# A scatter-add of expert results, with and without a bound on its row numbers

## The chip, the cores and the metric

The kernel runs on one core of a Trainium2 chip. The metric is the device time of one execution in microseconds (us), taken as the median of several runs. TensorE is called PE in the profile, VectorE DVE, ScalarE ACT, GpSimd POOL and SyncE SP; the core's transfers run on 16 DMA engines.

## The reference

One layer of a decoder is computed for 512 prompt tokens and 32 sample tokens, 544 tokens in all. The part that matters here is its end, a mixture of experts: every token goes to two of 32 experts, and the two results, times their gates, are added to the residual stream.

```python
    expert_ids = g_idx * EXPERTS_PER_GROUP + e_idx
    gates = jnp.einsum('nk,nke->ne', w, jax.nn.one_hot(expert_ids, N_EXPERTS, dtype=jnp.float32)).astype(h.dtype)
    y = jnp.zeros_like(h)
    for e in range(N_EXPERTS):
        hid = jax.nn.silu(h @ lw['w_expert_gate'][e]) * (h @ lw['w_expert_up'][e])
        y = y + gates[:, e:e + 1] * (hid @ lw['w_expert_down'][e])
    return y

def channel_mixer(x, lw):
    ...
    return x + hier_moe(h, lw).reshape(B, S, D)
```

So there are 1088 pairs of token and expert. With the inputs that the reference draws (seed 0) the 32 experts get between 20 and 53 of them each.

## The kernel before

The first 700 us compute the mixer (projections, attention, convolution, memory, output projection) and write the residual stream to `out_y_all` in HBM. Its last columns of work give the router's scores, from which the kernel builds tables: for every expert 64 slots (`CAP`), filled from slot 0 on with the tokens that chose it.

Then the experts run in a loop, `for e in range(NE)`. For each one SP loads its weights as six transfers of 1 MiB (`expert_w`: two for the gate matrix, two for up, two for down), into a ring of 23 buffers. `wload` lets at most four of them be in flight: each load waits for the one issued four before it (`DEPTH`), and also until its buffer is free. PE multiplies the 64 gathered token rows by the gate and up matrices (L1516), gathers the next expert's rows in between (L1330), transposes the hidden activations (L1530) and multiplies by the down matrix (L1536). The 1024 output columns are worked on as two halves, the first in partitions 0 to 63 and the second in partitions 64 to 127, so partition 64 f + s holds half f of slot s.

DVE multiplies the result by the gates into `o`, which is `work[:, :512]` (L1539). There is one such tile for all experts. GpSimd then issues one indirect DMA (L1540), which adds the 128 rows of `o`, 2 KB each, to rows of `y2`, the view of `out_y_all` in half rows. The row numbers stand in one column of the table `ids2`, built by `rows_of` (L1401 to L1406): a slot with token t gets rows 2 t and 2 t + 1, and an empty slot gets rows from 1088 on, which no output is made of (`YROWS = NT + CAP`, and the host takes the first `NT` rows only):

```python
    f["dummy"] = (NT + 1 + p % CAP).astype(np.float32)[:, None]
...
        V.tensor_scalar(idz, idf, 0.5, cfs("dummy"), op0=ALU.is_lt, op1=ALU.mult)
        V.tensor_tensor(idf, idf, idz, op=ALU.add)
        return V.tensor_scalar(ids2[:, at:at + n], idf, 2.0, cfs("half"), op0=ALU.mult, op1=ALU.add)
```

Each scatter waits for the one before it to land, since both add to the same tensor. After the loop a second one treats experts with more than 64 tokens; its number of turns is read from a table (L1618), and with these inputs it is zero.

Of the kernel before, what the change touches and what calls it, by code (L numbers as in the profile page):

```python
# [17 lines left out]
ALU = mybir.AluOpType  # L18
# [7 lines left out]
NT = NP + NS  # L26
# [126 lines left out]
def build(tc, I, O, cols):  # L153
# [44 lines left out]
    def nm(s):  # L198
        cnt[0] += 1
        return f"{s}_{cnt[0]}"  # L200
# [1298 lines left out]
    def expert(xT, w, gc, idc2, after=None, mid=None, early=None):  # L1499
        with tc.issue_after(after.ins) if after is not None else nullcontext():  # L1500
            return expert_mm(xT, w, gc, idc2, mid, early)
# [8 lines left out]
    def expert_mm(xT, w, gc, idc2, mid, early):  # L1510
        pgt = pm.tile([P, 256], F32, name=nm("pg"), tag="pg")
        pup = pm.tile([P, 256], F32, name=nm("pu"), tag="pu")
        for ps, ws in ((pgt, w[0:2]), (pup, w[2:4])):
            for k in range(8):
                for f in range(2):
                    last = nc.tensor.matmul(ps[CAP * f:CAP * f + CAP], xT[:, k, :], ws[k // 4][:, k % 4, 256 * f:256 * f + 256],  # L1516
                                     start=(k == 0), stop=(k == 7))
            if early is not None and ps is pgt:
                early(last)
        if mid is not None:  # L1520
            with tc.issue_after(last.ins):
                mid()
        hs = work[:, 512:768]
        nc.scalar.activation(hs, pgt, AF.Silu)
        hp_ = work[:, 768:1024].rearrange("p (k q) -> p k q", k=2)
        nc.vector.tensor_tensor(hp_.rearrange("p k q -> p q k"), hs.rearrange("p (q k) -> p q k", k=2),  # L1526
                                pup.rearrange("p (q k) -> p q k", k=2), op=ALU.mult)
        ph = pm.tile([P, 2, P], F32, name=nm("ph"), tag="ph", bufs=1)
        for k in range(2):
            nc.tensor.transpose(ph[:, k, :], hp_[:, k], ident)  # L1530
        hT = hs.rearrange("p (f s) -> p f s", f=2)
        nc.vector.tensor_copy(hT, ph)  # L1532
        pd = pm.tile([P, 512], F32, name=nm("pd"), tag="pd")
        for kk in range(4):
            for f in range(2):
                last = nc.tensor.matmul(pd[CAP * f:CAP * f + CAP], hT[:, kk % 2, CAP * (kk // 2):CAP * (kk // 2) + CAP],  # L1536
                                 w[4 + kk // 2][:, kk % 2, 512 * f:512 * f + 512], start=(kk == 0), stop=(kk == 3))
        o = work[:, :512]
        nc.vector.tensor_scalar(o, pd, gc, None, op0=ALU.mult)  # L1539
        nc.gpsimd.indirect_dma_start(out=y2, out_offset=bass.IndirectOffsetOnAxis(ap=idc2, axis=0), in_=o,  # L1540
                                     in_offset=None, compute_op=ALU.add)
        return last

    def overflow_tables():
# [141 lines left out]
```

## Time and profile before

| | us |
|---|---|
| median of three runs | 1209.25 (1209.0 to 1210.12) |
| the profiled execution | 1208.48 |
| span of its trace, first to last instruction | 1206.7 |
| experts' stage, first scatter to last | 739.18 to 1199.04 |
| span: busy PE | 1117.8 (93%) |
| span: busy POOL | 289.7 (24%) |

The profile counts 327.77 MB moved, 310.10 MB of them by the queue of SP and 14.62 MB by the queue of GpSimd, which the scatters use. An instruction that issues a DMA shows on its engine only while the engine deals with the issue; the transfer itself shows in the DMA share and in the time to landing. The chain of waits on the page ends at the conditional loop behind the experts and so names only the last scatter. The stage has to be read from stretches, from SP's issues and from the waits in them.

### The profile page before, as it was taken

What the parts mean: (1) busy time and instruction counts of PE and PEld (TensorE: products, weight loads), DVE (VectorE), ACT (ScalarE), POOL (GpSimd) and SP (SyncE); (2) the same over time, 40 slices, a digit from 0 to 9 for tenths busy, and PEclk for the clock granted to TensorE, in tenths of its full rate; (3) what the DMA queues carried; (4) which work ended last, traced back from release to release, by engine and by line L of the source; (5) the groups of instructions that cost most, each with busy time, mean ns of one, the idle gap of its engine ahead of it and who ended that gap; (6) DMA issues with size and microseconds to landing.
All of it is one profiled execution on the core that took longest, in us unless ns stands there. A gap on an engine that the chain in (4) does not pass through costs nothing. (4 is left out here: it accounts for less than half of the span.)

```text
span 1206.7 us, 21730 instructions
## 1 busy us (share of the span) xinstructions
PE 1117.8 (93%) x8965; PEld 827.2 (69%) x8965; DVE 526.2 (44%) x974; ACT 295.2 (24%) x723; POOL 289.7 (24%) x465
## 2 busy tenths in 40 slices
PE   6999999988389999999999998999999999888885
PEld 6998888987375899999998853555555555444442
DVE  6634444695475799856432264211225121111111
ACT  7434444422032432244332232000000000000000
POOL 4352434650068320222222000111111111001111
PEclk9999999999589999999999998999999999999999
DMA  9953100596967997212319179999999999999996
GB/s 322 230 149 90 48 34 27 215 367 179 271 238 256 397 358 248 86 61 80 140 68 378 71 279 395 403 404 401 398 402 404 404 404 404 403 402 404 402 404 238
DMA packets 116036, 327.77 MB, mean 272 GB/s; under 512 B 13353, under 2 KB 70257, under 8 KB 88032
## 3 DMA queue, kind: packets, MB, share of 16 engines
q1 hardware_dynamic: 105520, 310.10, 68.1%
q0 software_dynamic: 7664, 14.62, 5.4%
q10 hardware_dynamic: 2752, 1.65, 0.5%
q8 instruction: 71, 1.16, 0.4%
q14 instruction: 29, 0.24, 0.1%
HBM read 310.18 MB, written 31.49 MB: 283 GB/s over the span
## 5 line engine op out<-in xcount | busy, mean ns | idle before, releaser
L1540 POOL DMA_INDIRECT out_y_all<-work,ids x32 | 49.9, 1559 | 452.5 <-DVE work L1539 413.4
L694 PE MATMUL mm<-hTh,hi 128*128 128x272 f32 x512 | 150.2, 294 | 7.1 <-DVE u L745 6.0
L696 PE MATMUL mm<-hTh,lo 128*128 128x272 f32 x512 | 149.1, 292 | 0.0
L695 PE MATMUL mm<-hTl,hi 128*128 128x272 f32 x512 | 148.9, 291 | 0.0
L1516 PE MATMUL pu<-w,xgT 128*64 128x256 f32 x992 | 115.3, 381 | 14.6 <-DMA w<-in_w_expert_up 13.1
L1536 PE MATMUL pd<-w,work 128*64 128x512 f32 x512 | 118.2, 602 | 0.6 <-DVE work L1532 0.6
L1516 PE MATMUL pg<-w,xgT 128*64 128x256 f32 x992 | 114.6, 380 | 2.5 <-DMA w<-in_w_expert_gate 1.1
L1526 DVE TENSOR_TENSOR work<-work,pu 128x256 f32<-128x256 f32 x32 | 19.4, 608 | 210.5 <-PE pu L1516 210.5
L237 PE MATMUL mm<-hi,hTh 128*128 128x256 f32 x384 | 110.1, 287 | 0.0
L239 PE MATMUL mm<-hi,hTl 128*128 128x256 f32 x384 | 109.9, 286 | 0.0
L238 PE MATMUL mm<-lo,hTh 128*128 128x256 f32 x384 | 109.8, 286 | 0.0
L1516 PEld LDWEIGHTS pu<-w,xgT 128*64 128x64 f32 x992 | 69.3, 137 | 57.1 <-DMA w<-in_w_expert_up 22.0
L1516 PEld LDWEIGHTS pg<-w,xgT 128*64 128x64 f32 x992 | 70.3, 137 | 53.6 <-issue 15.9
L694 PEld LDWEIGHTS mm<-hTh,hi 128*128 128x128 f32 x512 | 97.8, 191 | 9.9 <-DVE u L745 6.4
L695 PEld LDWEIGHTS mm<-hTl,hi 128*128 128x128 f32 x512 | 97.9, 191 | 0.5 <-issue 0.4
L231 DVE TENSOR_TENSOR lo<-w,hi 128x2048 fp32r<-128x2048 f32 (+2 forms) x46 | 82.2, 1804 | 35.9 <-ACT hi L230 35.9
L696 PEld LDWEIGHTS mm<-hTh,lo 128*128 128x128 f32 x512 | 97.4, 191 | 0.4 <-issue 0.4
L715 DVE SCALAR_TENSOR_TENSOR cT<-u,cT 128x512 f32<-128x512 f32 x120 | 88.8, 763 | 1.3
L1330 PE MATMUL px<-h,ohs 64*64 64x512 f16 (+1 forms) x558 | 72.2, 387 | 5.1 <-DVE gates L1412 2.9
L1536 PEld LDWEIGHTS pd<-w,work 128*64 128x64 f32 x512 | 34.1, 137 | 62.3 <-issue 59.5
L1026 POOL TENSOR_TENSOR z<-z,gth 128x272 f32<-128x272 f32 x32 | 35.6, 1116 | 163.9 <-DVE gth L1025 163.9
L237 PEld LDWEIGHTS mm<-hi,hTh 128*128 128x128 f32 x384 | 72.4, 188 | 2.3 <-issue 2.2
(460 smaller groups left out, 2061.8 us busy)
## 6 DMA issues: line engine op xcount, KB each, us to landing
w<-in_w_expert_gate SPq DMA_DIRECT2D x64, 1024.0 KB, 11.1
w<-in_w_expert_up SPq DMA_DIRECT2D x64, 1024.0 KB, 10.6
w<-in_w_expert_down SPq DMA_DIRECT2D x64, 1024.0 KB, 11.1
w<-in_w_in SPq DMA_DIRECT2D x30, 512.0 KB, 7.3
w<-in_w_in SPq DMA_DIRECT2D x12, 1024.0 KB, 12.9
w<-in_cache_k SPq DMA_DIRECT2D x10, 1024.0 KB, 11.2
w<-q1d SPq DMA_DIRECT2D x8, 1024.0 KB, 11.2
out_k_win_sample<-in_cache_k SPq DMA_DIRECT2D x8, 1016.0 KB, 14.6
```

Of the source, the lines that this page charges most:

```text
L231: last_lo[0] = e.tensor_tensor(lo[:, s], v8(t)[:, s], hi[:, s].bitcast(F32), op=ALU.subtract)
L237: nc.tensor.matmul(ps, xh[k], wh[k], start=(k == 0), stop=False)
L238: nc.tensor.matmul(ps, xh[k], wl[k], start=False, stop=False)
L239: nc.tensor.matmul(ps, xl[k], wh[k], start=False, stop=(k == n - 1))
L694: nc.tensor.matmul(ps, wh[k], xh[k], start=(k == 0), stop=False)
L695: nc.tensor.matmul(ps, wh[k], xl[k], start=False, stop=False)
L696: nc.tensor.matmul(ps, wl[k], xh[k], start=False, stop=(k == n - 1))
L715: nc.vector.scalar_tensor_tensor(cTf[:, c, :NP], u[:, c, j:j + NP], w, cTf[:, c, :NP], op0=ALU.mult, op1=ALU.add)
L1330: nc.tensor.matmul(px[CAP * f:CAP * f + CAP], oh[:64 if i == 4 else P, i, :], src[:, 4 * f:4 * f + 4, :], start=(i == GORD[0] and r == 0), ...
L1516: last = nc.tensor.matmul(ps[CAP * f:CAP * f + CAP], xT[:, k, :], ws[k // 4][:, k % 4, 256 * f:256 * f + 256], start=(k == 0), stop=(k == 7))
L1536: last = nc.tensor.matmul(pd[CAP * f:CAP * f + CAP], hT[:, kk % 2, CAP * (kk // 2):CAP * (kk // 2) + CAP], w[4 + kk // 2][:, kk % 2, 512 * ...
L1540: nc.gpsimd.indirect_dma_start(out=y2, out_offset=bass.IndirectOffsetOnAxis(ap=idc2, axis=0), in_=o, in_offset=None, compute_op=ALU.add)
```

## The change

The indirect DMA gets a bound on its row numbers. Rows whose number is above `2 * NT - 1`, 1087, are to be left out of the transfer, and that is not to count as an error. All numbers of real rows lie from 0 to 1087 and all those of empty slots above, so what is left out are the additions to spare rows.

```diff
@@ -1538,7 +1538,7 @@
         o = work[:, :512]
         nc.vector.tensor_scalar(o, pd, gc, None, op0=ALU.mult)
         nc.gpsimd.indirect_dma_start(out=y2, out_offset=bass.IndirectOffsetOnAxis(ap=idc2, axis=0), in_=o,
-                                     in_offset=None, compute_op=ALU.add)
+                                     in_offset=None, bounds_check=2 * NT - 1, oob_is_err=False, compute_op=ALU.add)
         return last
```

No instruction is added, removed or moved on any of the five engines, and every wait stays; only names of buffers are numbered differently. The tables, the spare rows and the loop over overflowing experts stay as they are.

## Rows read from the trace of the kernel before

**Rows 1.** The page's slices: 40 equal parts of the span, tenths busy; GB/s moved.

```profile
PE   6999999988389999999999998999999999888885
PEclk9999999999589999999999998999999999999999
DMA  9953100596967997212319179999999999999996
GB/s 322 230 149 90 48 34 27 215 367 179 271 238 256 397 358 248 86 61 80 140 68 378 71 279 395 403 404 401 398 402 404 404 404 404 403 402 404 402 404 238
```

**Rows 2.** Stretches of the experts' stage: busy time by engine, PE clock, DMA share, GB/s.

```profile
core 0: us, PE busy (x) PEld busy (x) DVE busy (x) ACT busy (x) POOL busy (x), PEclk, DMA share, GB/s
739.00:1030.00 291.00, 282.59 (x2170) 149.34 (x2172) 68.38 (x147) 19.78 (x41) 32.82 (x21) 1.00 1.02 402
1030.00:1184.00 154.00, 136.48 (x986) 65.82 (x984) 27.37 (x48) 9.32 (x19) 14.04 (x10) 1.00 1.02 405
1184.00:1192.00 8.00, 6.15 (x54) 3.28 (x50) 0.00 (x0) 0.38 (x1) 1.45 (x1) 1.00 1.00 372
1192.00:1196.00 4.00, 2.62 (x14) 0.78 (x10) 1.02 (x2) 0.00 (x0) 0.00 (x0) 1.00 0.45 188
1196.00:1201.00 5.00, 1.94 (x8) 0.48 (x8) 0.75 (x1) 0.00 (x0) 1.57 (x1) 1.00 0.00 0
1201.00:1204.00 3.00, 0.00 (x0) 0.00 (x0) 0.00 (x0) 0.00 (x0) 0.00 (x0) 0.82 0.69 90
```

**Rows 3.** What SP's DMA queue waited for, 760 to 1190 us: total, times, longest.

```profile
SPq L579 <- DMA w<-in_w_expert_down: 127.0, 52, 3.3
SPq L579 <- DMA w<-in_w_expert_up: 119.5, 52, 3.7
SPq L579 <- DMA w<-in_w_expert_gate: 118.7, 52, 3.3
...
SPq L579 <- PE pg L1516: 1.1, 4, 0.4
SPq L579 <- PE pu L1516: 0.7, 3, 0.3
SPq L579 <- PE pd L1536: 0.5, 2, 0.2
SPq L579 <- PE px L1335: 0.4, 2, 0.2
SPq L579 <- PE px L1330: 0.2, 1, 0.2
```

**Rows 4.** SP's issues in order, two weight loads (1 MiB each) a row: start, us, what.

```profile
1106.58 3.05 SPq L579 DMA_DIRECT2D w<-in_w_expert_gate  x2
1112.74 2.84 SPq L579 DMA_DIRECT2D w<-in_w_expert_up  x2
1117.73 3.25 SPq L579 DMA_DIRECT2D w<-in_w_expert_down  x2
1122.84 3.06 SPq L579 DMA_DIRECT2D w<-in_w_expert_gate  x2
1129.01 2.82 SPq L579 DMA_DIRECT2D w<-in_w_expert_up  x2
1133.99 2.82 SPq L579 DMA_DIRECT2D w<-in_w_expert_down  x2
1138.97 3.08 SPq L579 DMA_DIRECT2D w<-in_w_expert_gate  x2
```

**Rows 5.** The scatters on GpSimd in order: start, us, what, and the idle time before.

```profile
739.18 1.75 POOL L1540 DMA_INDIRECT out_y_all<-work,ids  x1 [40.94 <-DVE work L1539]
754.91 1.59 POOL L1540 DMA_INDIRECT out_y_all<-work,ids  x1 [13.98 <-DVE work L1539]
768.97 1.57 POOL L1540 DMA_INDIRECT out_y_all<-work,ids  x1 [12.47 <-DVE work L1539]
...
1022.58 1.55 POOL L1540 DMA_INDIRECT out_y_all<-work,ids  x1 [12.51 <-DVE work L1539]
...
1103.18 1.55 POOL L1540 DMA_INDIRECT out_y_all<-work,ids  x1 [14.56 <-DVE work L1539]
1119.46 1.55 POOL L1540 DMA_INDIRECT out_y_all<-work,ids  x1 [14.73 <-DVE work L1539]
1135.73 1.55 POOL L1540 DMA_INDIRECT out_y_all<-work,ids  x1 [14.73 <-DVE work L1539]
...
1183.90 1.55 POOL L1540 DMA_INDIRECT out_y_all<-work,ids  x1 [13.86 <-DVE work L1539]
1199.04 1.57 POOL L1540 DMA_INDIRECT out_y_all<-work,ids  x1 [13.59 <-DVEq L1619]
```

**Rows 6.** Operations on out_y_all from 739 us on: durations, and issue to landing.

```profile
L1540 POOL DMA_INDIRECT out_y_all<-work,ids x32: 1547/1551/1745, 739.2 to 1199.0; - x32
...
DMA to landing us min/median/max: 5.0/9.6/10.5
```

**Rows 7.** The last expert's end, all engines in order of time.

```profile
1194.02 3.95 PE L1536 MATMUL pd<-w,work 128*64 128x512 f32 x16 [0.56 <-DVE work L1532]
...
1196.03 0.20 PEld L1536 LDWEIGHTS pd<-w,work 128*64 128x64 f32 x4 [0.96 <-DMA w<-in_w_expert_down]
...
1198.02 0.75 DVE L1539 TENSOR_SCALAR work<-pd,gates 128x512 f32<-128x512 f32 x1 [4.10 <-PE pd L1536]
```

**Rows 8.** The writes of the result tile on VectorE, two experts in a row.

```profile
1118.43 0.75 DVE L1539 TENSOR_SCALAR work<-pd,gates 128x512 f32<-128x512 f32 x1 [2.90 <-PE pd L1536]
...
1134.71 0.75 DVE L1539 TENSOR_SCALAR work<-pd,gates 128x512 f32<-128x512 f32 x1 [2.90 <-PE pd L1536]
```

**Rows 9.** The page's transfers by queue: packets, MB, share of the 16 engines' span.

```profile
q1 hardware_dynamic: 105520, 310.10, 68.1%
q0 software_dynamic: 7664, 14.62, 5.4%
```

## The prediction

> **What bounds the kernel now.** The change touches one line of the experts' stage, so I read from the whole to that stage. The page's slices [rows 1] show where: from slice 24 on the DMA engines are at 9 tenths or more and move about 400 GB/s to the end, while PE, which is busier over the whole span, falls to 8 tenths in the last third. The stretches say the same with numbers [rows 2]: from 739 to 1184 us the 16 DMA engines are busy for the whole time (share 1.02) in both halves, PE for 282.59 of 291 us in the first and for 136.48 of 154 us in the second. What feeds them is SP's queue: its waits from 760 to 1190 us [rows 3] are 365 us on the landing of earlier weight loads (156 waits) and about 3 us on PE, so buffers are free nearly always and the queue of four loads is always full. In the first half PE keeps its own pace of 14.06 us an expert (754.91 to 768.97) from a stock of loaded weights, and once the stock is used up it follows the loads, 16.3 us an expert [rows 5].
>
> So the stream of loads sets the end from 739 us on, also where PE is the busier engine: the last loads land when the stream is done, and the last expert's second half of the down product waits for its weights [rows 7]. A saving in DMA time anywhere in the stage is worth its full size at the end, until PE's own pace takes over. That is far: from 1022.58 us eleven more experts at 14.06 us would put the last scatter at 1177.2 instead of 1199.04 [rows 5], some 22 us.
>
> **What a scatter costs.** SP issues the loads in pairs, and each row of its list starts when loads issued four earlier have landed. In [rows 4] the starts are 6.16, 4.99, 5.11, 6.17, 4.98 and 4.98 us apart: two loads of 1 MiB take 4.98 us where nothing else moves, and one interval in three takes 6.165. One scatter goes out in each such period, so the scatter costs the stream 6.165 - 4.98 = 1.18 us. By its bytes alone, 256 KB at the loads' rate, it would be a quarter of 2.49, 0.62 us; adding to rows costs about twice the bytes. Scatters of the first 31 experts lie in the stream (739.18 to 1183.90 us); the 32nd runs behind it, alone. 31 times 1.18 is **36.6 us** that the stream spends on scatters.
>
> **What the change takes away.** 1088 of the 2048 slots hold a token, so 47% of the rows are left out, 17% to 69% by expert. Instructions and waits stay, so nothing else is to be summed: POOL's issue takes 1551 ns and stands before 12 to 15 us of idle time [rows 5, 6], and a longer or shorter issue is hidden unless it delays the landing by several us (a rival below). Rows left out cost between nothing and all that they cost now; I take nothing, as the word "left out" says, and keep the other end for the range.
>
> How much of the 36.6 us goes depends on one thing that no row shows: how the 128 rows are dealt to the 16 engines. A load is landed when its last part is, so the engine with the fullest share of scatter rows paces the stream. Slots are filled from 0 up, so the empty ones all lie at the end of each half. Three deals:
> - even: every engine loses 47%. The gain is 0.47 x 36.6 = 17.2 us.
> - mixed: an engine's eight rows come from places far apart in the 64 slots. If it takes every sixteenth row, the engine with slots 0, 16, 32 and 48 keeps 162 of its 248 rows over the 31 experts (17 experts have over 32 tokens, 3 over 48), and 35% go, 12.7 us. With two groups of four rows, 32 apart, the engine of slots 0 to 3 and 32 to 35 keeps 180 of 248, and 27% go, 10.0 us.
> - in blocks: an engine takes eight neighbouring rows. All experts have at least 20 tokens, so the engines of slots 0 to 15 keep every row, and nothing is gained.
>
> The ends are 0 and 17.2 us. I take the mixed deal, the middle of its two cases: 31%, **11.3 us**. The even deal would need the rows that are left to be dealt anew after the empty ones are dropped, a step more than leaving them out; blocks are the other plain way to cut 128 rows, and I find no row against them.
>
> [...]
>
> [...] The rows say 1.18 us for a scatter. [...]
>
> **The tail.** The last scatter's rows move alone, in 1201 to 1204 us at a share of 0.69 [rows 2]. Its expert has 39 tokens, so the fullest engine loses one row in eight or none: at most 0.3 us, left out of the sum. The profiled execution took 1208.48 us, 1.78 more than its span, and 0.77 less than the median of 1209.25, from which I subtract: 1209.25 - 11.3 = 1197.95, so **1198.0**.
>
> **Rivals.**
> - *Even deal*: 1209.25 - 17.2 = 1192.0. For it: one would expect dropped rows to relieve all engines. Against it: the fixed order of the slots. PE's pace would still be 4 us away.
> - *No gain*: rows in blocks, or the bound not acting on an adding transfer, or a left-out row that still takes its turn: 1209.3. For it: the two fullest eighths of the slots have no empty one, and the change has no other lever. [...]
> - *Half-way*: the mixed deal with left-out rows that still cost a fifth to four fifths of a full one: a gain of 2.3 to 9.0 us, 1200 to 1207.
> - *Slower*: testing each number against the bound makes GpSimd slower at setting up the rows. The result tile is single, so the next write of it (L1539) has to wait for the scatter to land, and PE behind that. Now a landing takes 9.6 us, at most 10.5 [rows 6], and the tile is written again 15.25 us after the issue (1119.46 to 1134.71) [rows 5, 8]: at least 4.7 us of slack there. Bound in this way, an expert takes landing + 0.75 + 0.27 us (the write and the step to the issue). The stage's mean is (1199.04 - 739.18) / 31 = 14.83 us, so it decides from a landing of 13.8 us on. At 14.5 us it would be 15.52 x 31 = 481 instead of 460 us, a time of 1230. Against it: the setting up would have to grow by over 4 us, nearly three times what the issue takes now.
>
> **Chances.** A change of 0.2% is 2.4 us, about what a measurement of this kernel can tell from none. Mixed deal 0.42, even deal 0.18, half-way 0.08: faster 0.68. No gain: same 0.25. Slower 0.07. The range goes from the even deal, with one us for the reading of 1.18, to no gain with the spread of the runs: 1191.0 to 1210.5. The mixed deal alone is 1196.5 to 1199.3.
>
> **What would show it.** If rows are left out, GpSimd's queue moves 14.62 MB [rows 9] less 47% of the 8.39 MB of the 32 scatters (128 rows of 2 KB each), 10.7 MB. The interval with a scatter in SP's list falls from 6.165 to about 5.8 us (mixed), 5.6 (even) or stays (blocks), that without stays at 4.98. In the mixed and the block case the DMA share of the stage falls below 1.0, since the emptier engines wait for the fullest; in the even case it stays. PE's pace of 14.06 us holds for more experts than before, and the issue to landing stays below 10.5 us. The prediction is wrong if the bytes fall and the interval doesn't, if the landing goes beyond 13.8 us, or if SP begins to wait for PE.

## The result, and the profile after

The changed kernel takes 1193.39 us (median of four runs, 1193.04 to 1194.43) beside 1209.26 us for the kernel before: a ratio of 0.9869 with a 95% interval of 0.9857 to 0.9882, a gain of 15.9 us. The forecast was 1198.0 in a range of 1191.0 to 1210.5. The direction and the place are right; the gain is 4.6 us larger than the 11.3 us of the sum, outside the 1196.5 to 1199.3 of the mixed deal and 1.4 us from the 1192.0 of the even one.

Two lines of the changed kernel's page, all packets with their sizes and GpSimd's queue (packets, MB, share of 16 engines), the second beside [rows 9]:

```profile
DMA packets 116036, 323.85 MB, mean 272 GB/s; under 512 B 15273, under 2 KB 72177, under 8 KB 88032
...
q0 software_dynamic: 7664, 10.70, 3.8%
```

GpSimd's queue moves 10.70 MB instead of 14.62, as forecast for 47% of the scatters' 8.39 MB. Its packets are as many as before, 7664: a left-out row does not disappear but becomes a packet of a few bytes (the 1920 rows left out, 2 KB each, are 3.93 MB, and the queue moves 3.92 MB less). The count "under 512 B" says so too. It was 13353 before and is 15273 now, 1920 more, and the two halves of the 960 empty slots are 1920 rows.

Stretches of the experts' stage in the columns of [rows 2]:

```profile
739.00:1030.00 291.00, 282.83 (x2174) 149.78 (x2174) 68.89 (x148) 19.76 (x41) 32.81 (x21) 1.00 1.02 411
1030.00:1168.00 138.00, 130.51 (x972) 66.44 (x972) 27.06 (x47) 9.30 (x19) 13.94 (x9) 1.00 1.01 404
1176.00:1180.00 4.00, 2.67 (x22) 1.35 (x20) 1.02 (x2) 0.00 (x0) 0.00 (x0) 1.00 0.42 149
```

Up to 1168 us the DMA share is 1.02 and 1.01 and PE is busier than before in its second half, 130.51 of 138 us. The loads end earlier. Their end, the second half of the last down product waiting for its weights, is this row of the timeline, beside 1196.03 in [rows 7]:

```profile
1180.97 0.28 PEld L1536 LDWEIGHTS pd<-w,work 128*64 128x64 f32 x4 [0.58 <-DMA w<-in_w_expert_down]
```

That is 15.1 us earlier. The profiled execution took 1193.17 us, with a span of 1191.4 beside 1206.7. Of the scatters, beside [rows 5]:

```profile
740.50 1.74 POOL L1540 DMA_INDIRECT out_y_all<-work,ids  x1 [42.25 <-DVE work L1539]
...
1066.05 1.55 POOL L1540 DMA_INDIRECT out_y_all<-work,ids  x1 [12.52 <-DVE work L1539]
1080.12 1.55 POOL L1540 DMA_INDIRECT out_y_all<-work,ids  x1 [12.51 <-DVE work L1539]
1094.18 1.55 POOL L1540 DMA_INDIRECT out_y_all<-work,ids  x1 [12.52 <-DVE work L1539]
1108.24 1.55 POOL L1540 DMA_INDIRECT out_y_all<-work,ids  x1 [12.51 <-DVE work L1539]
1122.38 1.55 POOL L1540 DMA_INDIRECT out_y_all<-work,ids  x1 [12.59 <-DVE work L1539]
...
1184.06 1.57 POOL L1540 DMA_INDIRECT out_y_all<-work,ids  x1 [12.34 <-DVEq L1619]
```

The stage begins 1.3 us later than before and its last scatter comes 15.0 us earlier; what lies behind it is about the same, 7.3 us to the end of the span beside 7.7. PE keeps its own pace of some 14.06 us up to the scatter at 1122.38, where before it lost it after 1022.58. SP still waits for the landing of loads and hardly for PE (total us, times, longest; beside [rows 3]):

```profile
SPq L579 <- DMA w<-in_w_expert_down: 118.1, 52, 3.2
...
SPq L579 <- PE pg L1516: 1.2, 4, 0.3
```

So the whole gain lies in the stream of loads. SP's list, beside [rows 4], shows how it comes:

```profile
1067.40 2.81 SPq L579 DMA_DIRECT2D w<-in_w_expert_up  x2
1072.94 2.81 SPq L579 DMA_DIRECT2D w<-in_w_expert_down  x2
1077.91 2.83 SPq L579 DMA_DIRECT2D w<-in_w_expert_gate  x2
1082.90 2.82 SPq L579 DMA_DIRECT2D w<-in_w_expert_up  x2
1089.12 2.79 SPq L579 DMA_DIRECT2D w<-in_w_expert_down  x2
1094.07 2.82 SPq L579 DMA_DIRECT2D w<-in_w_expert_gate  x2
1099.06 3.54 SPq L579 DMA_DIRECT2D w<-in_w_expert_up  x2
1104.75 3.13 SPq L579 DMA_DIRECT2D w<-in_w_expert_down  x2
1109.73 2.82 SPq L579 DMA_DIRECT2D w<-in_w_expert_gate  x2
1115.29 2.81 SPq L579 DMA_DIRECT2D w<-in_w_expert_up  x2
...
1125.25 2.94 SPq L579 DMA_DIRECT2D w<-in_w_expert_gate  x2
1131.44 2.80 SPq L579 DMA_DIRECT2D w<-in_w_expert_up  x2
```

Two loads with nothing else still take 4.95 to 4.99 us. The interval with a scatter, 6.165 before, now has different lengths. The five scatters from 1066.05 to 1122.38 belong to experts 23 to 27 with 20, 46, 37, 27 and 53 tokens, and the intervals behind their issues are 5.54, 6.22, 5.69, 5.56 and 6.19 us. With 20 or 27 tokens the price is halved, from 1.18 to 0.56 and 0.58 us; with 46 or 53 it is the old one, though 28% and 17% of the rows are left out. So the price does not fall in step with the rows. A fixed deal in which every engine has four rows of the first 32 slots and four of the last 32, the second of the prediction's mixed cases, would give these four prices; which engine carries a row the trace does not show. The expert with 37 tokens is the odd one: by that deal the engines of slots 0 to 3 and 32 to 35 would have all eight rows, and yet it costs only 0.71 us (5.69 - 4.98). Those of the second group, slots 4 to 7 and 36 to 39, would have five rows of eight, and five eighths of 1.18 are 0.74 us: the second group's share fits, the first group's does not.

### The profile page after: what moved, and what is told of

Read it like the earlier page. It is cut to its first block, busy times and chain, and to the rows that moved or that the text cites. A ratio compares the mean times of both kernels' runs of the same rounds, so it can differ in the third digit from the quotient of the medians.

```text
span 1191.4 us, 21761 instructions
## 1 busy us (share of the span) xinstructions
PE 1112.9 (93%) x8964; PEld 827.6 (69%) x8965; DVE 526.5 (44%) x974; ACT 294.9 (25%) x723; POOL 291.4 (24%) x465
## 2 busy tenths in 40 slices
DMA packets 116036, 323.85 MB, mean 272 GB/s; under 512 B 15273, under 2 KB 72177, under 8 KB 88032
## 3 DMA queue, kind: packets, MB, share of 16 engines
q0 software_dynamic: 7664, 10.70, 3.8%
## 5 line engine op out<-in xcount | busy, mean ns | idle before, releaser
L1540 POOL DMA_INDIRECT out_y_all<-work,ids x32 | 49.9, 1558 | 437.5 <-DVE work L1539 399.7
## 6 DMA issues: line engine op xcount, KB each, us to landing
w<-q1d SPq DMA_DIRECT2D x8, 1024.0 KB, 11.3
```

## Experiments

Where a kernel changes only a table of constants, the diff shows that line.

**A bound that leaves nothing out.**

```diff
-                                     in_offset=None, bounds_check=2 * NT - 1, oob_is_err=False, compute_op=ALU.add)
+                                     in_offset=None, bounds_check=2 * YROWS - 1, oob_is_err=False, compute_op=ALU.add)
```

> The changed kernel with the bound raised to the last spare row, 2 * YROWS - 1, so that no row is left out and all additions are made as before. It tells the bound itself from the rows that it leaves out. Theory (the gain of 15.9 us is DMA time of rows left out): the time of the kernel before, 1209 us, within 2 us, and 14.62 MB in GpSimd's queue. Rival (asking for a bound moves GpSimd or the transfer to another, quicker way): about 1193 us as in the changed kernel.

Measured: 1209.11 us beside 1208.88, ratio 1.0005 (0.9995 to 1.0015). GpSimd's queue on its page is that of before:

```profile
q0 software_dynamic: 7664, 14.62, 5.4%
```

The bound itself costs and gives nothing; the gain comes from the rows left out.

**Another order of filling the slots.** The table `iota64` says which token number a slot takes, in the gather, in the tables of row numbers and in the gates, so one line deals the tokens anew. In the even deal the tokens go to the eight groups of slots (four slots and the four 32 further on) in turn:

```diff
-    f["iota64"] = np.tile(np.arange(1, 65, dtype=np.float32), (P, 1))
+    sl = np.arange(CAP)
+    f["iota64"] = np.tile((1 + 8 * (4 * (sl // 32) + sl % 4) + sl % 32 // 4).astype(np.float32), (P, 1))
```

> The changed kernel with the tokens of an expert dealt to its slots in another order: token number r goes to the eight groups of slots (four slots and the four that lie 32 further on) in turn, so that the real rows are spread over all groups; nothing else differs and all is computed. Theory A (fixed deal, an engine takes four neighbouring rows and four more 32 further on; the engine with most real rows paces the loads): the fullest engine keeps 145 of 248 rows over 31 scatters instead of 180, the gain over the kernel before grows from 15.9 to between 17 and 20 us, a time of 1189 to 1192. Theory B (rows that are left get dealt anew, or only their number counts): as many rows are left out as in the changed kernel, so the same 1193.4 within 1 us. Theory C (every sixteenth row to an engine): the fullest engine gets about the same share as now, 1193 within 2 us. The bytes are those of the changed kernel, 10.70 MB, in all cases.

Measured: 1191.06 us beside 1208.88, ratio 0.9854 (0.9838 to 0.9871), a gain of 17.8 us. The scatters of the experts with 20, 46 and 37 tokens in SP's list (issued at 1065.69, 1079.75 and 1093.81):

```profile
1067.04 2.82 SPq L580 DMA_DIRECT2D w<-in_w_expert_up  x2
1072.42 2.82 SPq L580 DMA_DIRECT2D w<-in_w_expert_down  x2
...
1082.39 2.82 SPq L580 DMA_DIRECT2D w<-in_w_expert_up  x2
1088.27 2.79 SPq L580 DMA_DIRECT2D w<-in_w_expert_down  x2
...
1098.22 3.56 SPq L580 DMA_DIRECT2D w<-in_w_expert_up  x2
1103.93 3.11 SPq L580 DMA_DIRECT2D w<-in_w_expert_down  x2
```

The intervals are 5.38, 5.88 and 5.71 us: the expert with 46 tokens has got 0.34 us cheaper than in the changed kernel, at the same number of rows. Dealt in turn, the fullest groups of these three experts hold 3, 6 and 5 rows of eight. By 1.18 us for eight that is 0.44, 0.89 and 0.74 us, and above 4.98 the intervals lie by 0.40, 0.90 and 0.73.

The packed deal is the opposite order, eight tokens to a group before the next group is begun:

```diff
+    sl = np.arange(CAP)
+    f["iota64"] = np.tile((1 + 8 * (sl % 32 // 4) + 4 * (sl // 32) + sl % 4).astype(np.float32), (P, 1))
```

> As the even deal, with the opposite order: the first eight tokens of an expert fill the first group of slots (0 to 3 and 32 to 35), the next eight the second group, and so on. All is computed. Theory A: the first two groups hold real rows in all 31 scatters, their engines lose nothing, and the gain is only what these engines had in hand over the slowest one in the kernel before, 0 to 5 us: 1204 to 1209. Theory B: as the changed kernel, 1193.4 within 1 us. Theory C (every sixteenth row): an engine then takes rows of four groups, and the gain stays near that of the changed kernel, 1191 to 1198.

Measured: 1209.14 us beside 1208.88, ratio 1.0003 (0.9993 to 1.0012). As many rows are left out as in the changed kernel, and nothing at all is gained. SP's list has the old intervals again, 6.05 us for the expert with 20 tokens (its scatter is issued at 1070.43) and 6.17 for the one with 46 (at 1085.45):

```profile
1072.80 2.82 SPq L580 DMA_DIRECT2D w<-in_w_expert_gate  x2
1078.85 2.94 SPq L580 DMA_DIRECT2D w<-in_w_expert_up  x2
...
1088.95 3.22 SPq L580 DMA_DIRECT2D w<-in_w_expert_gate  x2
1095.12 2.79 SPq L580 DMA_DIRECT2D w<-in_w_expert_up  x2
```

This kernel and the even deal differ in one table and lie 18 us apart. Packets (7664 of GpSimd's queue in both), bytes (10.70 MB), instructions and waits are the same, so it matters in which slots the rows that stay lie; theories B and C (rows dealt anew, every sixteenth row) fall. Theory A's groups fit, though no trace shows its engines. One thing did not come as forecast: the DMA share does not fall below 1.0. In this stretch it is 1.01, with 398 GB/s beside 405 in [rows 2]. The rows left out, 3.92 MB in a stage of 460 us, are 8.5 GB/s by themselves, so the loads move as before:

```profile
1030.00:1184.00 154.00, 137.83 (x988) 66.72 (x986) 27.37 (x47) 9.32 (x19) 15.50 (x10) 0.99 1.01 398
```

**The order alone, without a bound** (the kernel before with the table of the even deal).

> The kernel before, without a bound, with the slot order of the even deal. It tells whether the order alone, through the gather or the tables, moves the time. Every theory on the scatter's rows: 1209 us within 2 us, since all 128 rows are added. Rival (the order itself helps): a gain of 1 us or more over the kernel before, which then has to be taken off the even deal's.

Measured: 1208.44 us beside 1208.88, ratio 0.9998 (0.9988 to 1.0007). The order does nothing by itself.

**The first two groups exchanged**, to find out why 27%, the share of the fullest group, gave 15.9 us instead of 10.0.

```diff
+    sl = np.arange(CAP)
+    f["iota64"] = np.tile((1 + np.where(sl % 32 < 8, sl ^ 4, sl)).astype(np.float32), (P, 1))
```

> The changed kernel with the first two groups of slots exchanged in the order in which tokens fill them: the first four tokens go to slots 4 to 7, the next four to slots 0 to 3, and likewise 36 to 39 before 32 to 35. All is computed, and as many rows are left out. The fullest share (180 of 248 rows) now falls to the second group, and the first has 158. The prediction's sum gave 10.0 us for this deal and 15.9 were measured. Theory A (the engines of the first group run some 4 to 6 us ahead of the slowest over the stage, and the slowest is in the second group with 158 rows): now the slowest has 180, the gain falls to 10 to 12 us, a time of 1197 to 1199. Theory B (all engines alike, a row costs more than the 1.18 us for 128 of them said): nothing changes, 1193.4 within 1 us.

Measured: 1198.37 us beside 1209.14, ratio 0.9916 (0.9903 to 0.9930), a gain of 10.8 us. With the fullest share in the second group the gain is what the sum had for the fullest share; with it in the first group it is 5 us more. So the eight groups are not alike, and in the changed kernel the time does not go by the fullest. SP's list shows it in one scatter, that of the expert with 37 tokens (issued here at 1095.41). Now the second group has all eight rows and the first has five:

```profile
1098.81 3.06 SPq L580 DMA_DIRECT2D w<-in_w_expert_gate  x2
1104.96 2.84 SPq L580 DMA_DIRECT2D w<-in_w_expert_up  x2
```

The interval is 6.15 us, the full price, where the changed kernel has 5.69 with the same rows in the other order.

**The price of a row.** Every fourth slot gets a number above the bound, in these lines of the constants (the same bound at the last spare row here and in the next three):

```diff
-    f["half"] = (p // CAP - 2).astype(np.float32)[:, None]
+    out = p % 4 == 3
+    f["half"] = (p // CAP - 2 + 4096 * out).astype(np.float32)[:, None]
```

> Scatter with a bound at the last spare row, in which every fourth slot (3, 7, 11 and so on) gets a number above the bound, whether a token is in it or not; those rows of the result are missing from the output. Every group of four slots loses one row, so each engine makes 6 of 8 additions in each scatter, and nothing else is uneven. It measures the price of a row where all engines lose the same. By 1.18 us a scatter, a quarter of it 31 times: a gain of 9.1 us, 1199.8. If a scatter costs an engine 1.38 us (some 1.85 for two rows of eight would be the other end): 10.7 us, 1198.2. Theory B wants a price of 1.8 us or more: a gain of 14 us, 1195.

Measured: 1199.40 us beside 1209.14, ratio 0.9913 (0.9898 to 0.9928), a gain of 9.7 us (8.7 to 12.3 by the interval). A quarter of the rows in 31 scatters makes 9.7 / (31 / 4) = 1.26 us for a whole scatter, beside the 1.18 read from SP's list. SP's list of this run agrees: behind the scatters from 1082.55 to 1145.61 the intervals are 5.83 to 5.89 us, 0.85 to 0.91 for three quarters of the rows, so 1.13 to 1.21 for all. The price of the prediction stands; a price of 1.8 us, with which equal engines would have explained the 15.9, does not.

**One group kept, all others left out.**

```diff
+    out = p // 4 % 8 != 0
```

> Scatter with a bound at the last spare row, in which only slots 0 to 3 and 32 to 35 of each half are added and all other rows get a number above the bound; the other rows of the result are missing from the output. The engines of the first group work as in the kernel before, all others lose the scatter. What the time falls is what the first group's engines have in hand over the slowest. Theory A: 4 to 6 us, 1203 to 1205. Theory B: 0 to 1 us, 1208 to 1209.

Measured: 1210.27 us beside 1209.14, ratio 1.0003 (0.9991 to 1.0014). Nothing is gained, as if the first group paced like any other. The interval behind a scatter is the full one; for the scatter issued at 1075.48 it is 6.22 us (in the profiled execution, the slowest of ten at 1214.25 us):

```profile
1078.76 3.11 SPq L580 DMA_DIRECT2D w<-in_w_expert_gate  x2
1084.98 2.83 SPq L580 DMA_DIRECT2D w<-in_w_expert_up  x2
```

Then the second group, `out = p // 4 % 8 != 1`:

> The same with slots 4 to 7 and 36 to 39 kept instead; the other rows of the result are missing from the output. Theory A: the slowest engine is in the second group, so nothing is gained, 1208 to 1209. Theory B: 0 to 1 us as well. If it gains as much as the first group's run or more, the slowest engine is in neither group and theory A falls.

Measured: 1215.64 us beside 1209.14, ratio 1.0058 (1.0042 to 1.0073), slower by 6.5 us. Theory A said 4 to 6 us of gain for the first and none for the second. The difference between the two, 5.4 us, is as large as it said, but both lie some 6 us higher, so the runs do not bear it out. Here seven eighths of the scatters' rows are gone and the kernel is not faster, or is slower, than with all of them. All transfers together move at 385 GB/s in the stage's second half, beside 405 in [rows 2], but some 16 of these 20 GB/s are the rows themselves (GpSimd's queue moves 7.31 MB less over the 460 us), so this line alone does not show slower transfers:

```profile
1030.00:1184.00 154.00, 134.81 (x973) 65.40 (x973) 26.49 (x46) 9.30 (x19) 13.95 (x9) 0.99 1.00 385
```

**All rows left out**, `out = p >= 0`, to tell whether left-out rows do that.

> All numbers of rows are set above the bound, so every scatter is issued, tests its 128 numbers and adds nothing; the experts' part is missing from the output. It measures two things: how far PE's own pace lets the time fall, and whether left-out rows do harm of their own. The prediction put PE's limit some 22 us below the kernel before: 1187, while the stream alone would allow 31 times 1.2 us or more, 1171. If left-out rows cost nothing: 1185 to 1189, with SP waiting for PE. Rival, raised by the run that kept only the second group and came out 6.5 us above the kernel before: the many tiny left-out rows hold up the transfers: 1195 or more.

Measured: 1183.25 us beside 1209.09, ratio 0.9792 (0.9775 to 0.9808), a gain of 25.8 us. The packets are as many as ever, and 4096 more of them than before are under 512 B, all 128 rows of 32 scatters:

```profile
DMA packets 116036, 319.41 MB, mean 271 GB/s; under 512 B 17449, under 2 KB 74353, under 8 KB 88032
q0 software_dynamic: 7664, 6.27, 1.8%
```

SP's list has lost the third interval: nearly all are about 5.0 us (two of 6.5 aside).

```profile
1102.44 2.82 SPq L580 DMA_DIRECT2D w<-in_w_expert_down  x2
1107.43 2.83 SPq L580 DMA_DIRECT2D w<-in_w_expert_gate  x2
```

So a left-out row costs the stream nothing that can be read. The scatters keep PE's pace, 14.06 us, until the last expert:

```profile
768.62 1.57 POOL L1541 DMA_INDIRECT out_y_all<-work,ids  x1 [12.47 <-DVE work L1540]
782.68 1.55 POOL L1541 DMA_INDIRECT out_y_all<-work,ids  x1 [12.50 <-DVE work L1540]
...
1175.19 1.57 POOL L1541 DMA_INDIRECT out_y_all<-work,ids  x1 [10.78 <-DVEq L1620]
```

That is the limit by PE, which the prediction had put some 22 us below the kernel before; it is 26, and below the expected 1185 to 1189. SP does not wait for PE, as was expected: the loads run on and are simply done early, the last pair being issued at 1147.56, 27.6 us before the last scatter, beside 16.6 us in the kernel before. By themselves the tiny rows are not what made the runs with one group slow.

**The second group kept, with eight loads in flight.**

```diff
-DEPTH = 4
+DEPTH = 8
```

> The run that kept only slots 4 to 7 and 36 to 39 (the other rows of the result are missing from the output), with eight weight loads in flight instead of four. It was 6.5 us slower than the kernel before although its busiest engines do the same work. Theory D (with four loads in flight the engines that have nothing else to do start each new load together, in a rush, and hold up the one that is behind; with eight they run ahead and the rush ends): back to 1207 to 1211. Theory E (the full engine is slower whenever the others carry only loads, whatever the queue): 1213 to 1218 as before.

Measured: 1237.66 us beside 1209.09, ratio 1.0233 (1.0210 to 1.0257). The run decides nothing between D and E, because the edit changed more than the queue: the order of VectorE's instructions is another one. In every other kernel here VectorE writes the result tile (L1540) as soon as PE's down product is done (a wait of 2.90 us on it in [rows 8]). Here the write stands behind later experts' work. The third expert's down product ends at 768.73 and its result is written at 779.86, after the fourth expert's L1527 at 775.76; with four loads in flight it is written at 768.74. PE keeps 14.07 us an expert up to its sixth down product (765.08, 779.15, 793.22, 807.28), and from the next one on it has to wait for these late writes, as here:

```profile
1158.06 0.61 DVE L1527 TENSOR_TENSOR work<-work,pu 128x256 f32<-128x256 f32 x1 [10.73 <-PE pu L1517]
...
1162.16 0.74 DVE L1540 TENSOR_SCALAR work<-pd,gates 128x512 f32<-128x512 f32 x1
1162.96 0.20 PEld L1537 LDWEIGHTS pd<-w,work 128*64 128x64 f32 x4 [1.68 <-DVE work L1540]
1162.96 3.65 PE L1537 MATMUL pd<-w,work 128*64 128x512 f32 x16 [1.44 <-DVE work L1540]
```

So PE is held up by VectorE, its buffers come free late, and SP waits for PE for some 116 us between 760 and 1160, beside 4 us in the run with four loads in flight. The largest of these waits (total us, times, longest):

```profile
SPq L580 <- PE pd L1537: 67.5, 24, 6.4
```

What a longer queue alone does to this kernel is not known from it.

**The even deal and the changed kernel again, side by side.**

> The kernel of the even deal once more, beside the changed kernel on the same chip, to compare the two. By the fullest share in the slowest group (142 rows of 248 instead of 158) and 0.157 us a row of an engine: 2.5 us below the changed kernel, near 1191.

> The changed kernel itself, as the other half of that comparison: 1193.4 within 1 us, a gain of about 15.9 us over the kernel before.

Measured: even deal 1191.17 us (1190.26 to 1192.93), ratio 0.9855 (0.9838 to 0.9871); changed kernel 1193.05 us (1192.28 to 1193.78), ratio 0.9870 (0.9853 to 0.9886). The even deal's median is lower by 1.9 us here and by 2.3 us between the earlier runs of the two. The intervals of the ratios overlap, so the lead is likely and not proved; it is the fastest of the kernels that compute everything.

## Why the prediction was right, and where it was not

- **The bound.** Right. The loads set the end: the interval between loads changed only where a scatter lies, the last load came 15.1 us earlier and the whole kernel 15.9. With all rows gone the time fell by 25.8 us and then stood at PE's pace. The 22 us of the prediction were too few: the last expert, which has no next expert to gather for, takes 1.7 us less than 14.06, and with no rows to land the span ends 5.4 us behind the last scatter instead of 7.7.
- **The price.** Right. 1.18 us a scatter, from one interval in three, against 1.26 (1.12 to 1.59 by the interval) where it was measured by itself. By its bytes at the rate of the loads it would have been half of that, 0.62 us (an estimate from 4.98 us for two loads), and the even deal would have given some 9.0 us (0.47 of 31 times that); the runs gave 15.9 and 17.8.
- **What is left out costs nothing.** Right for a scatter of which nothing is added, as the run without any additions shows. The packets stay, as packets of a few bytes.
- **The deal.** Right in kind. The packed order gains nothing, the even order the most, at equal bytes. That an engine carries two groups of four rows, 32 apart, was the prediction's assumption, and no trace shows it; the runs show 1209.1 us with the tokens packed into these groups and 1191.1 with the groups filled in turn. The other term of the 11.3, the deal by every sixteenth row, no run shows: with it the packed order was to take 1191 to 1198 us, and it took 1209.1. The rival of blocks is out: it gave no gain for the change, which gained 15.9 us, and in the even deal, which gained 17.8, the engine of slots 0 to 7 would keep nearly all rows. (Of the prediction's counts one is off without effect: 17 of all 32 experts have over 32 tokens, 16 of the 31, and the sum of 162 rows uses 16.)
- **The step that failed: the term of the deal was mis-sized.** "The engine with the fullest share of scatter rows paces the stream" takes the 16 engines for equals. With the fullest share in the second group the rule gives 27% and 10.8 us were measured; with it in the first group, as in the change, 15.9. What comes nearest is the second group's own share, 158 of 248 rows: 36% of 36.6 to 39.0 us (1.18 and 1.26 a scatter) is 13.3 to 14.1 us, beside 15.9 (14.3 to 17.3 by the interval); 142 of 248 in the even deal makes 15.6 to 16.7, beside 17.8 (15.6 to 19.6); 248 of 248 in the packed deal makes nothing, beside -0.3. The first two sums still fall 1 to 3 us short, and where that comes from is not shown. The scatter of the expert with 37 tokens says the same without a sum: 5.69 us with five rows in the second group, 6.15 with eight. Taking the middle of two deals, 11.3, hid the error: the case whose groups fit the runs had 10.0, the gap is nearly 6 us, and that 11.3 came nearer is luck. The range held the result because it reached as far as the even deal.
- **Why the first group did not set the pace in the change** is not settled. The theory that its engines run ahead of the others was tested straight, by keeping one group, and not borne out: with the first group alone nothing is gained, and its scatters cost the full interval. That this run is 5.4 us faster than the one with the second group proves little, since the latter is slower than the kernel before for a cause that is open.
- **What would show it.** The bytes, the interval at 4.98 and the landing, 8.9 us with at most 9.9, came as said. The interval with a scatter was to fall to one value, and it depends on the expert instead. The DMA share was to fall below 1.0 and did not: it is 1.01 here, and 1.01 in the packed deal too, where as many rows are left out and nothing is gained, so it does not tell the cases apart. The landing of the scatters beside [rows 6]:

```profile
L1540 POOL DMA_INDIRECT out_y_all<-work,ids x32: 1547/1551/1744, 740.5 to 1184.1; - x32
...
DMA to landing us min/median/max: 4.7/8.9/9.9
```

- **Rivals.** By its time alone the change, 1193.4, would have spoken for the even deal (1192.0), which had 0.18, rather than for the mixed one. The table of slots decides: with as many rows left out the same kernel takes 1191.1 dealt in turn and 1209.1 packed, which an even deal of what is left cannot do. No gain (1209.3) is out by the 15.9 us, and the half-way case by the run without any additions. The slower case has no sign: POOL's issue takes the same 1551 ns.

## What to carry to other kernels

Where the transfers set the end, price a small one by the interval between the large ones, with it and without it, rather than by its bytes: 1.18 us here beside an estimated 0.62. Look at which rows of a scatter fall away, not only how many: as many are left out in the packed order, 1209.1 us, as in the even one, which spreads those that stay over all groups, 1191.1. When an edit is to test one thing, see in the trace that the order of the instructions has stayed; here eight loads in flight instead of four changed it. A one-line change to a table of slots moved 18 us at equal bytes.

## What was not expected of the hardware

- A row number above the bound leaves a packet of a few bytes behind (1920 more packets under 512 B in the change, 4096 with all rows left out), which cost the loads nothing to be seen: 5.0 us for a pair of loads with 128 of them in between.
- The first two groups of slots differ: exchanging which of them carries the fullest share moved the gain from 15.9 to 10.8 us.
- A scatter of which only the second group of slots is added was slower than one with all rows, 1215.6 beside 1209.1 us. The cause is open.
